# Encoder layer on one core: one VectorE instruction with the inverse rms, the shift inside the split, and the first instructions in another order

## The chip, the core and the metric

The kernel runs on one core of a Trainium2 chip. A core has TensorE (PE, the matrix unit; it loads 128x128 weights, which a profile shows as PEld, and writes to PSUM), VectorE (DVE), ScalarE (ACT), GpSimd (POOL) and SyncE (SP), whose queue issues all DMAs of this kernel. Each engine takes its instructions in the order of the program and waits on semaphores for the others. The metric is the device time of one execution in microseconds (us), lower is better.

## What is computed

One encoder layer for two groups of 1024 tokens, "prompt" and "sample", with 1024 channels, in fp32:

```python
mod = silu(c) @ w_ada + b_ada
shift, scale, gate = split(mod, 3)
h = rms_norm(x, norm_g) * (1.0 + scale) + shift          # the "modulated" rows
qa, ka, va, za, qb, kb, vb, zb, ga, gb = split(h @ w_in)
oa = gqa_attention(rope(rms_norm(qa)), rope(rms_norm(ka)), va) * silu(za)
ob = rms_norm(diff_attention(qb, kb, vb, lam)) * (1 - lam_init) * silu(zb)
merged = sigmoid(ga) * (oa @ w_proj_a) + sigmoid(gb) * (ob @ w_proj_b)
out = x + gate * (merged @ w_out)
```

`rms_norm(x)` is `x * rsqrt(mean(x*x) + eps) * g`. Scale and shift are one number per channel and group; the inverse rms is one number per token.

## The kernel before

**Layout and split.** The rows `x` come transposed: a tile holds 128 channels (a chunk, c = 0 to 7) by 512 tokens (`hf` = 0 or 1, the first or second half rows). Every fp32 matmul is made of three matmuls on numbers of reduced precision (fp32r): each operand is split into a high part (a ScalarE copy that rounds) and a low part (value minus high part), and hi·hi, hi·lo and lo·hi are added in PSUM. So `ht[hf]` is two lists of chunks, high and low, and a weight tile `w` has a high and a low half, made by `split_w`: ScalarE copies, then GpSimd subtracts, or VectorE for every other piece while `alone[0]` is true (outside attention).

**Start of the first group (`start`).** The modulation is made on PE out of eight 1 MB pieces of `w_ada` (`ada`, L324; the sum lies in a PSUM tile). `ada_end` copies a sum to SBUF (VectorE, L342), lays it out by channels with eight small matmuls (`laid`, L336), adds the bias (L348) and, for the scale, multiplies by norm_g (L352): the result is `modc`. There are four such sums: shift and scale of chunks 0 to 3, shift and scale of chunks 4 to 7. The inverse rms of the first half rows comes from squares (ScalarE, L272), sums on VectorE (L278 to L283), a matmul with ones and a power on GpSimd (`inv_rms`), and is spread over all partitions by `spread` (four transposes on PE, L308, and a copy on ScalarE, L310). Then the rows are multiplied by it (L394), scaled and shifted (`modulated`: L360 on VectorE or L358 on ScalarE), copied to the high part (L363) and subtracted for the low part (L364). The squares of the second half rows follow.

**Head.** `kva_gen` makes k and v of branch A for one tile of 128 tokens at a time (24 matmuls of 128x256, L539; then rms and rope of the row on VectorE, and a transpose of the row on PE, L593, two tiles later), and `z_gen` makes one z tile (24 matmuls of 128x512, L709). Tiles 0 to 3 use the first half rows, tiles 4 to 7 the second. `head` sets the order for the first group: tiles 0 and 1, one z tile, `late()` (inverse rms, spread and modulation of the second half rows, `start_late`: L412, L415, L416, L417), tiles 2 and 3, a second z tile, then the rest woven with query projections. After that attention and projections are woven by a table of shares.

**Second group.** `ht_gen` modulates the rows of the second group chunk by chunk, woven with the output projection `out_gen` of the first (L977): two VectorE instructions (L515), one GpSimd addition of the shift (L518), two high copies (L523) and two subtractions (L524) per chunk.

**What sets the order.** The code is written for all engines in one sequence; a scheduler then places each engine's instructions by its own estimate of times. `behind(a, b)` pins a behind b on one engine, and `tc.high_priority` raises some. A tile pool with a number of buffers makes a writer wait for the last reader of the buffer: `spool` has 3 buffers for weight pieces (`st`), `mtile("ev")` has one.

Of the kernel before, what the change touches and what calls it, by code (L numbers as in the profile page):

```python
# [12 lines left out]
F32 = mybir.dt.float32  # L13
F32R = mybir.dt.float32r
AF = mybir.ActivationFunctionType
# [5 lines left out]
P = 128  # L21
# [37 lines left out]
LAG = 2  # L59

# [28 lines left out]
def kernel(ctx: ExitStack, tc: tile.TileContext, t: dict):  # L89
# [99 lines left out]
    def split_w(w, q, st):  # L189
        wh = w[:, q * 2 : q * 2 + 2, 0, :]  # L190
        wl = w[:, q * 2 : q * 2 + 2, 1, :]
        nc.scalar.activation(wh, st, AF.Copy)  # L192
        e = nc.vector if alone[0] and q % 2 else nc.gpsimd
        e.tensor_tensor(out=wl, in0=st, in1=wh.bitcast(F32), op=ALU.subtract)  # L194

    def split_early(what):
        w, sts = what
        for q, st in enumerate(sts):
            split_w(w, q, st)
# [69 lines left out]
    def squares(xT):  # L269
        sq = [pair().rearrange("p (c n) -> p c n", c=4) for _ in range(2)]  # L270
        for c in range(NCH):
            nc.scalar.activation(sq[c // 4][:, c % 4], xT[c], AF.Square)  # L272
        return sq
# [30 lines left out]
    def spread(rs):  # L304

        bank = gbank()
        for k in range(4):
            nc.tensor.transpose(bank[:, k * P : (k + 1) * P], rs[:, k : k + 1].to_broadcast([P, P]), ident)  # L308
        rsb = mtile("ev", [P, 512], bufs=1)
        nc.scalar.activation(rsb, bank, AF.Copy)  # L310
        return rsb
# [26 lines left out]
    def ada_end(n):  # L338
# [3 lines left out]
        nc.vector.tensor_copy(row, acc)  # L342
# [8 lines left out]
        if third:  # L351
            nc.vector.tensor_tensor(out=mc, in0=mc, in1=gcol[:, cs].unsqueeze(2).to_broadcast(both), op=ALU.mult)  # L352

    def modulated(ht, hf, xT, cs):
        for c in cs:
            scale, shift = modc[:, 1, c, 0:1], modc[:, 0, c, 0:1]
            if c % 4 > 1:
                nc.scalar.activation(xT[c], xT[c], AF.Identity, scale=scale, bias=shift)  # L358
            else:
                nc.vector.tensor_scalar(  # L360
                    out=xT[c], in0=xT[c], scalar1=scale, scalar2=shift, op0=ALU.mult, op1=ALU.add
                )
            nc.scalar.activation(ht[hf][0][c], xT[c], AF.Copy)  # L363
            end = nc.vector.tensor_tensor(  # L364
                out=ht[hf][1][c], in0=xT[c], in1=ht[hf][0][c].bitcast(F32), op=ALU.subtract
            )
        return end
# [9 lines left out]
    def start(ht):  # L377
# [10 lines left out]
        for n in range(8):  # L388
            ada(n, wts[n])
            if n == 3:  # L390
                rsb = spread(inv_rms(added(squares(xT[0]))))
                for c in range(NCH):
                    e = nc.gpsimd if c % 3 == 2 else nc.vector
                    e.tensor_tensor(out=xT[0][c], in0=xT[0][c], in1=rsb, op=ALU.mult)  # L394
            if n in (2, 4, 6, 7):
                ada_end(n if n == 7 else n - 1)
            if n == 4:
                add_h(ht, 0, 0)
                modulated(ht, 0, xT[0], range(4))
        split_early(kva_w[0])  # L400
        add_h(ht, 0, 1)
        end = modulated(ht, 0, xT[0], range(4, 8))
        sq = squares(xT[1])
        return lambda: start_late(ht, xT, inv_rms(added(sq, end), latest[0]))

    def start_late(ht, xT, rs):
        rsb = spread(rs)
        for c in range(NCH):
            x = xT[1][c]
            if c % 4 == 0:  # L410
                add_h(ht, 1, c // 4)
            nc.vector.scalar_tensor_tensor(  # L412
                out=x, in0=x, scalar=modc[:, 1, c, 0:1], in1=rsb, op0=ALU.mult, op1=ALU.mult
            )
            nc.scalar.activation(x, x, AF.Identity, bias=modc[:, 0, c, 0:1])  # L415
            nc.scalar.activation(ht[1][0][c], x, AF.Copy)  # L416
            nc.vector.tensor_tensor(out=ht[1][1][c], in0=x, in1=ht[1][0][c].bitcast(F32), op=ALU.subtract)  # L417
# [71 lines left out]
    def ht_gen(g, ht):  # L489
# [20 lines left out]
        for c in range(NCH):  # L510
            xt = ptile()
            dma(xt, xT_in[g][c * P : (c + 1) * P])
            for hf in range(2):
                xh = xt[:, hf * 512 : (hf + 1) * 512]
                nc.vector.scalar_tensor_tensor(  # L515
                    out=xh, in0=xh, scalar=modc[:, 1, c, g : g + 1], in1=rsb[hf], op0=ALU.mult, op1=ALU.mult
                )
            nc.gpsimd.tensor_scalar(  # L518
                out=xt, in0=xt, scalar1=modc[:, 0, c, g : g + 1], scalar2=1.0, op0=ALU.add, op1=ALU.mult
            )  # L520
            for hf in range(2):
                xh = xt[:, hf * 512 : (hf + 1) * 512]
                nc.scalar.activation(ht[hf][0][c], xh, AF.Copy)  # L523
                nc.vector.tensor_tensor(out=ht[hf][1][c], in0=xh, in1=ht[hf][0][c].bitcast(F32), op=ALU.subtract)  # L524
# [465 lines left out]
    def head(g, st, zs, late):  # L990
# [3 lines left out]
        if g == 0:  # L994

            for i in range(2):
                drain(islice(kva, 6))
                drain(islice(zs, 3))
                if i == 0:
                    late()  # L1000
# [179 lines left out]
```

## Time and profile before

| | us |
|---|---|
| median of 3 runs | 1931.95 (1931.21 to 1932.6) |
| the profiled execution, its own time | 1934.43 |
| its span | 1932.7 |
| PE busy | 1863.8 |
| VectorE busy | 1161.5 |
| ScalarE busy | 760.0 |
| GpSimd busy | 674.2 |

A row of a timeline gives start, duration, engine, line, operation, output and inputs by the program's names, the count of merged instructions and, in brackets, how long the engine idled before and who released it. A row of windows gives the stretch, then busy time (count) of PE, its weight loads, VectorE, ScalarE and GpSimd, then PE's granted clock as a share of full speed, the DMA share and GB/s. The duration of a merged row runs from the first start to the last end.

### The profile page before, as it was taken

How to read it: one execution, taken by the hardware profiler on the slowest of the kernel's cores; microseconds unless marked ns; L12 is line 12 of the kernel's file. 1: busy time of each engine (PE TensorE's matmuls, PEld its weight loads, DVE VectorE, ACT ScalarE, POOL GpSimd, SP SyncE). 2: the span in 40 equal slices, each digit the busy share in tenths (PEclk: the TensorE clock that was granted, in tenths of full speed). 3: DMA queues.
4: the chain of work that ended last, by engine and by line, in shares of the span. 5: the costliest groups of instructions: out<-in, count | busy, mean ns of one | idle time of the engine just before them, and what ended most of it. 6: DMA issues, size and time to landing. Idle time of an engine off the chain costs nothing. (4 is left out here: it accounts for less than half of the span.)

```text
span 1932.7 us, 29441 instructions
## 1 busy us (share of the span) xinstructions
PE 1863.8 (96%) x10434; PEld 1562.7 (81%) x10434; DVE 1161.5 (60%) x1709; ACT 760.0 (39%) x1548; POOL 674.2 (35%) x912
## 2 busy tenths in 40 slices
PE   6989999999999998999999999999999899999999
PEld 3778878888888996788888777888888798877887
DVE  5787663444667366757467777445357736666731
ACT  4444442444445344323233455234445524442210
POOL 2233421433456254121222434024456616322110
PEclk8999999999999999999999999999999999999999
DMA  8136674546243355875631567564525423587531
GB/s 316 54 87 172 182 200 133 156 128 201 81 137 100 98 169 156 268 259 179 209 104 50 166 183 198 157 180 132 163 78 143 111 79 90 157 251 248 170 103 55
DMA packets 268883, 295.03 MB, mean 153 GB/s; under 512 B 35136, under 2 KB 217536, under 8 KB 268736
## 3 DMA queue, kind: packets, MB, share of 16 engines
q1 hardware_dynamic: 268736, 293.15, 51.0%
q8 instruction: 83, 1.36, 0.3%
q14 instruction: 64, 0.52, 0.1%
HBM read 133.59 MB, written 42.01 MB: 91 GB/s over the span
## 5 line engine op out<-in xcount | busy, mean ns | idle before, releaser
L709 PE MATMUL f<-u,w 128*128 128x512 f32 x2256 | 588.4, 398 | 1.3 <-ACT w L192 0.9
L539 PE MATMUL f<-w,u 128*128 128x256 f32 x3456 | 484.0, 286 | 1.9 <-DVE ev L719 0.9
L709 PEld LDWEIGHTS f<-u,w 128*128 128x128 f32 x2256 | 415.2, 190 | 85.2 <-issue 2.7
L539 PEld LDWEIGHTS f<-w,u 128*128 128x128 f32 x3456 | 456.8, 192 | 24.2 <-issue 2.7
L745 DVE TENSOR_REDUCE m<-s 128x1 f32<-128x1024 f32 x256 | 309.9, 1218 | 208.3 <-PE s L744 205.9
L746 ACT ACTIVATE p<-s,m 128x1024 f32<-128x1024 f32 x256 | 285.2, 1115 | 287.4 <-DVE m L745 219.2
L194 POOL TENSOR_TENSOR w<-st,w 128x512 fp32r<-128x512 f32 x168 | 223.0, 1345 | 455.9 <-ACT w L192 415.4
L787 DVE STREAM_TRANSPOSE p<-p 128x1024 f32<-128x1024 f32 x192 | 237.0, 1240 | 69.0 <-ACT p L746 59.3
L560 POOL TENSOR_TENSOR rs<-ss,nhalf 128x4 f32<-128x4 f32 (+1 forms) x112 | 109.1, 975 | 361.7 <-DVE ss L559 317.8
L744 PE MATMUL s<-u,sw 128*128 128x512 f32 x512 | 204.8, 400 | 0.0
L192 ACT ACTIVATE w<-st 128x512 fp32r<-128x512 f32 x196 | 115.1, 626 | 147.1 <-DMA st<-in_w_in_dram 92.2
L946 PE MATMUL f<-u,w 128*128 128x512 f32 x552 | 137.4, 398 | 3.9 <-DVE u L957 3.2
L819 PE MATMUL a<-q,u 128*128 128x256 f32 x512 | 132.8, 394 | 8.0 <-DMA q<-p 5.5
L946 PEld LDWEIGHTS f<-u,w 128*128 128x128 f32 x552 | 103.7, 190 | 27.4 <-DVE u L957 4.8
L819 PEld LDWEIGHTS a<-q,u 128*128 128x128 f32 x512 | 98.6, 198 | 24.9 <-issue 5.9
L802 PE MATMUL a<-q,u 128*64 128x256 f32 x1024 | 117.6, 382 | 1.0 <-DMA q<-p 1.0
L743 PE MATMUL s<-u 128*128 128x512 f32 x256 | 108.0, 422 | 10.2 <-ACT p L746 8.9
L596 DVE TENSOR_TENSOR u<-f,u 64x256 fp32r<-64x256 f32 (+1 forms) x196 | 80.6, 411 | 58.1 <-ACT u L595 53.1
L743 PE MATMUL s<-u,u 128*128 128x512 f32 x256 | 104.9, 410 | 8.4 <-DVE ev L719 4.3
L744 PEld LDWEIGHTS s<-u,sw 128*128 128x128 f32 x512 | 97.4, 190 | 17.5 <-issue 0.8
L977 PE MATMUL f<-u,w 128*128 128x512 f32 x456 | 105.6, 389 | 0.0
L786 DVE SCALAR_TENSOR_TENSOR p<-p,r,p 128x1024 f32<-128x1024 f32 x64 | 87.2, 1362 | 28.8 <-POOL r L772 24.2
(168 smaller groups left out, 1939.7 us busy)
## 6 DMA issues: line engine op xcount, KB each, us to landing
q<-p SPq DMA_DIRECT2D x768, 128.0 KB, 2.6
st<-in_w_in_dram SPq DMA_DIRECT2D x132, 256.0 KB, 3.1
zd<-ev SPq DMA_DIRECT2D x96, 256.0 KB, 2.6
sw<-u SPq DMA_DIRECT2D x256, 64.0 KB, 2.0
p<-zd SPq DMA_DIRECT2D x64, 256.0 KB, 4.1
u<-in_w_ada_dram SPq DMA_DIRECT2D x8, 1024.0 KB, 11.4
od<-oo SPq DMA_DIRECT2D x64, 128.0 KB, 2.4
st<-in_w_in_dram SPq DMA_DIRECT2D x64, 128.0 KB, 2.8
```

The source lines that it names most:

```text
L192: nc.scalar.activation(wh, st, AF.Copy)
L194: e.tensor_tensor(out=wl, in0=st, in1=wh.bitcast(F32), op=ALU.subtract)
L539: ins = nc.tensor.matmul(ps, lt[c][:, sl], w[:, c, wi, :], start=(k == 0), stop=(k == 23))
L709: ins = nc.tensor.matmul(ps, w[:, c, wi, e * P : (e + 1) * P], rt[c], start=(k == 0), stop=(k == 23),)
L743: nc.tensor.matmul(s[:, sl], q, k[:, sl], start=True, stop=False)
L744: nc.tensor.matmul(s[:, sl], sw, k[:, sl], start=False, stop=True)
L745: nc.vector.tensor_reduce(out=m, in_=s, axis=AX.X, op=ALU.max, negate=True)
L746: nc.scalar.activation(pt.rearrange("p (j c a) -> p j c a", j=4, c=8), s.rearrange("p (c a j) -> p j c a", c=8, j=4), AF.Exp, bias=m, accu ...
L787: nc.vector.transpose(pt, pt)
L802: lambda k=k, m=m: nc.tensor.matmul(acc[(LO, HI)[m]], u["v"][:, k], pT[m][:, k], start=(k == 0), stop=(k == 7))
L819: nc.tensor.matmul(acc, u["v"][:, k], pT[:, k], start=(k == 0), stop=(k == 7))
L946: nc.tensor.matmul(ps, w[:, c, wi, d * P : (d + 1) * P], o[:, oi, :], start=(k == 0), stop=(k == 11))
```

## The change

For every chunk and half, `modulate` writes three instructions that are bound to the engines' order: on VectorE x * scale * inverse rms in one instruction; on ScalarE the high part, rounded out of x + shift; on VectorE the low part, (x + shift) - high part. The low part of a chunk is pinned behind the next chunk's first instruction. It takes the place of `modulated` and the loop L394 in `start`, of the loop in `start_late`, and of the loops in `ht_gen`. The shift is no longer added by an instruction of its own.

Besides, `late` is now two steps (`FIRST`): the inverse rms of the second half rows behind the first z tile, their spread and modulation behind tiles 2 and 3; the spread is pinned behind the last matmul written before it, z matmuls included. The squares of the second half rows are pinned two by two behind the high parts of the first half's chunks 4 to 7, and the VectorE splits of the k/v weights behind the last copy of the modulation sums.

```diff
+FIRST = (("kva", 6), ("z", 3), ("late", 0), ("kva", 6), ("late", 1), ("z", 3))
...
-    def split_w(w, q, st):
+    def split_w(w, q, st, after=None):
...
-        e.tensor_tensor(out=wl, in0=st, in1=wh.bitcast(F32), op=ALU.subtract)
+        ins = e.tensor_tensor(out=wl, in0=st, in1=wh.bitcast(F32), op=ALU.subtract)
+        if after is not None and e is nc.vector:
+            behind(ins, after)
...
-    def squares(xT):
+    def squares(xT, after=None):
...
+            if after is not None:
+                behind(ins, after[c // 2])
...
-    def spread(rs):
+    def spread(rs, after=None):
...
+            if after is not None:
+                behind(ins, after)
...
-    def modulated(ht, hf, xT, cs):
...
+    def modulate(ht, hf, xs, rsb, g=0):
+
+        acts = []
+
+        def low(c, x):
+            hi, lo = (part[c] for part in ht[hf])
+            return nc.vector.scalar_tensor_tensor(
+                out=lo, in0=x, scalar=modc[:, 0, c, g : g + 1], in1=hi.bitcast(F32), op0=ALU.add, op1=ALU.subtract
+            )
+
+        prev, ins = None, None
+        for c, x in xs + [(None, None)]:
+            if x is not None:
+                new = nc.vector.scalar_tensor_tensor(
+                    out=x, in0=x, scalar=modc[:, 1, c, g : g + 1], in1=rsb, op0=ALU.mult, op1=ALU.mult
+                )
+                if ins is not None:
+                    behind(new, ins)
+                ins = new
+                acts.append(nc.scalar.activation(ht[hf][0][c], x, AF.Identity, bias=modc[:, 0, c, g : g + 1]))
+            if prev:
+                new = low(*prev)
+                behind(new, ins)
+                ins = new
+            prev = c, x
+        return ins, acts
...
                 rsb = spread(inv_rms(added(squares(xT[0]))))
-                for c in range(NCH):
-                    e = nc.gpsimd if c % 3 == 2 else nc.vector
-                    e.tensor_tensor(out=xT[0][c], in0=xT[0][c], in1=rsb, op=ALU.mult)
             if n in (2, 4, 6, 7):
-                ada_end(n if n == 7 else n - 1)
+                copied = ada_end(n if n == 7 else n - 1)
             if n == 4:
                 add_h(ht, 0, 0)
-                modulated(ht, 0, xT[0], range(4))
-        split_early(kva_w[0])
+                modulate(ht, 0, list(enumerate(xT[0]))[:4], rsb)
+        split_early(kva_w[0], copied)
         add_h(ht, 0, 1)
-        end = modulated(ht, 0, xT[0], range(4, 8))
-        sq = squares(xT[1])
-        return lambda: start_late(ht, xT, inv_rms(added(sq, end), latest[0]))
+        end, acts = modulate(ht, 0, list(enumerate(xT[0]))[4:], rsb)
+        sums = added(squares(xT[1], acts), end)
+        rs = []
+        return lambda: rs.append(inv_rms(sums, latest[0])), lambda: start_late(ht, xT, rs[0])

     def start_late(ht, xT, rs):
-        rsb = spread(rs)
...
+        rsb = spread(rs, latest[0])
+        for half in range(2):
+            add_h(ht, 1, half)
+            modulate(ht, 1, list(enumerate(xT[1]))[half * 4 : half * 4 + 4], rsb)
...
                         if col == C_ZA and hf == e == k == 0 and alone[0]:
                             behind(ins, latest[0])
+                        if alone[0]:
+                            latest[0] = ins
```

Line numbers after the change lie a few to some twenty lines further on (L342 is L349, L348 and L352 are L355 and L359, L194 is L195, L539 is L540, L709 is L710, L308 is L313, L310 is L317); L375 is the new first instruction, L381 the high part and L368 the low part.

On VectorE in `start`, before, between the first copy of a modulation sum (`p` from PSUM `s` or `f`) and the modulation of chunks 4 to 7 (`u_168`; `u_167` holds chunks 0 to 3, `ev_253` the spread inverse rms, `u_278` the low parts):

```order
L342 COPY p_268<-s_207 128x512
L394 TENSOR_TENSOR u_167<-u_167,ev_253 128x512 x3
L394 TENSOR_TENSOR u_168<-u_168,ev_253 128x512 x3
L348 TENSOR_TENSOR modc<-s_270,bcol 128x8
L342 COPY p_300<-f_263 128x512
L352 TENSOR_TENSOR modc<-modc,gcol 128x8
L360 TENSOR_SCALAR u_167<-u_167,modc 128x512 x2
L364 TENSOR_TENSOR u_278<-u_167,u_277 128x512 x3
L348 TENSOR_TENSOR modc<-f_302,bcol 128x8
L364 TENSOR_TENSOR u_278<-u_167,u_277 128x512
L194 TENSOR_TENSOR w_185<-p_186,w_185 128x2x256
L342 COPY p_312<-f_295 128x512
```

and the same place now (`u_270` holds the low parts, `w_185` is the k/v weight):

```order
L355 TENSOR_TENSOR modc<-s_262,bcol 128x8
L359 TENSOR_TENSOR modc<-modc,gcol 128x8
L375 SCALAR_TENSOR_TENSOR u_167<-u_167,modc,ev_253 128x512 x2
L349 COPY p_292<-f_255 128x512
L368 SCALAR_TENSOR_TENSOR u_270<-u_167,modc,u_269 128x512
L375 SCALAR_TENSOR_TENSOR u_167<-u_167,modc,ev_253 128x512
L368 SCALAR_TENSOR_TENSOR u_270<-u_167,modc,u_269 128x512
L375 SCALAR_TENSOR_TENSOR u_167<-u_167,modc,ev_253 128x512
L368 SCALAR_TENSOR_TENSOR u_270<-u_167,modc,u_269 128x512 x2
L355 TENSOR_TENSOR modc<-f_294,bcol 128x8
L349 COPY p_304<-f_287 128x512
L195 TENSOR_TENSOR w_185<-p_186,w_185 128x2x256
```

The six multiplications are gone from in front of the scale's sum, and the weight splits (the second one comes next) stand behind the last copy of a sum, where one stood ahead of it.

On PE, before, from the end of the first z tile (`f_461`) to tiles 2 and 3 (`f_548`, `f_595`); `row_…` are rows to be transposed, `rs_501` is the inverse rms of the second half rows:

```order
L291 MATMUL s_495<-ones_c,q_343 128x1 x4
L709 MATMUL f_461<-u_329,w_444 128x512 x2
L709 MATMUL f_461<-u_330,w_444 128x512
L709 MATMUL f_461<-u_329,w_444 128x512
L593 MATMUL s_636<-ident,row_428 128x128
L308 MATMUL f_505<-ident,rs_501 128x128 x4
L539 MATMUL f_548<-w_185,u_277 128x256 x2
L539 MATMUL f_548<-w_185,u_278 128x256
```

and now, in the middle of the second z tile (`f_626`; tile 2 is done before the first z tile ends, tile 3 behind it):

```order
L710 MATMUL f_626<-u_270,w_440 128x512
L710 MATMUL f_626<-u_269,w_440 128x512
L313 MATMUL s_591<-ident,rs_493 128x128 x4
L710 MATMUL f_626<-u_321,w_440 128x512
L710 MATMUL f_626<-u_322,w_440 128x512
```

The spread of the second half rows' inverse rms has moved from ahead of tiles 2 and 3 to behind the 12th matmul of the second z tile. Behind that tile, on PE now, tiles 4 (`f_656`) and 5 (`f_703`) begin, which use the second half rows (`u_598` high, `u_599` low):

```order
L594 MATMUL s_697<-ident,row_522 128x128
L540 MATMUL f_656<-w_185,u_598 128x256 x2
L540 MATMUL f_703<-w_185,u_598 128x256 x2
L540 MATMUL f_656<-w_185,u_599 128x256
L540 MATMUL f_656<-w_185,u_598 128x256 x2
L540 MATMUL f_703<-w_185,u_599 128x256
L540 MATMUL f_703<-w_185,u_598 128x256 x2
L540 MATMUL f_656<-w_185,u_599 128x256
L540 MATMUL f_703<-w_185,u_599 128x256
L540 MATMUL f_656<-w_185,u_598 128x256 x2
L540 MATMUL f_703<-w_185,u_598 128x256 x2
L540 MATMUL f_656<-w_185,u_599 128x256
```

Both tiles go through the chunks together, and the last row of these is the low part of chunk 2.

On VectorE now, the modulation of the second half rows (`u_192` and `u_193` hold chunks 0 to 3 and 4 to 7, `u_599` and `u_613` the low parts), behind the rope of tile 3 (`row_569`):

```order
L375 SCALAR_TENSOR_TENSOR u_192<-u_192,modc,ev_596 128x512 x2
L375 SCALAR_TENSOR_TENSOR u_193<-u_193,modc,ev_596 128x512 x2
L583 TENSOR_TENSOR row_569<-rc_580,row_569 128x128
L368 SCALAR_TENSOR_TENSOR u_599<-u_192,modc,u_598 128x512
L375 SCALAR_TENSOR_TENSOR u_192<-u_192,modc,ev_596 128x512
L368 SCALAR_TENSOR_TENSOR u_599<-u_192,modc,u_598 128x512
L375 SCALAR_TENSOR_TENSOR u_192<-u_192,modc,ev_596 128x512
L597 TENSOR_TENSOR u_356<-s_697,u_356 64x128
L368 SCALAR_TENSOR_TENSOR u_613<-u_193,modc,u_612 128x512
```

The two halves of four chunks are interleaved: chunks 0, 1, 4 and 5 are multiplied before the first low part, and the low part of chunk 2 comes behind 6 and 7.

More of the change, by code (lines that the diff above doesn't have):

```diff
@@ L352, in ada_end @@
             nc.vector.tensor_tensor(out=mc, in0=mc, in1=gcol[:, cs].unsqueeze(2).to_broadcast(both), op=ALU.mult)
[L354 to L367 removed]
+        return ins
+    def modulate(ht, hf, xs, rsb, g=0):
[10 more added lines that the diff above has]
+                    out=x, in0=x, scalar=modc[:, 1, c, g : g + 1], in1=rsb, op0=ALU.mult, op1=ALU.mult
+                )
+                if ins is not None:
[8 more added lines that the diff above has]
+        return ins, acts
     kva_w = []
@@ L513, in ht_gen @@
             for hf in range(2):
[L514 to L524, printed above, removed]
+                modulate(ht, hf, [(c, xt[:, hf * 512 : (hf + 1) * 512])], rsb[hf], g)
             yield 1
@@ L994, in head @@
         if g == 0:
[L996 to L1000, printed above, removed]
+            for what, n in FIRST:
+                if what == "late":
+                    late[n]()
+                else:
+                    drain(islice(kva if what == "kva" else zs, n))
             weave((chain(kva, qa), 40, 0.0), (islice(zs, nz - 6), nz - 6, Z_HEAD_A[g]))
```

20 lines of the change are left out of this document (5 added, 15 removed).

## The prediction

> **What bounds the kernel.** I read the page first, then busy time by windows, then the timelines of TensorE, VectorE and ScalarE over the first 90 us and around 990 us.
>
> ```profile
> PE 1863.8 (96%) x10434; PEld 1562.7 (81%) x10434; DVE 1161.5 (60%) x1709; ACT 760.0 (39%) x1548; POOL 674.2 (35%) x912
> 30.00:40.00 10.00, 6.03 (x27) 4.31 (x28) 7.79 (x15) 7.26 (x14) 3.25 (x2) 0.51 1.08 358
> 50.00:60.00 10.00, 7.07 (x33) 5.43 (x34) 7.54 (x27) 2.71 (x4) 4.04 (x5) 0.87 0.43 136
> 90.00:100.00 10.00, 10.00 (x73) 9.40 (x72) 6.32 (x19) 3.76 (x11) 3.49 (x4) 1.00 0.43 132
> 990.00:1000.00 10.00, 10.00 (x70) 9.30 (x69) 5.59 (x9) 3.43 (x9) 4.90 (x4) 1.00 0.30 104
> ```
>
> TensorE (PE) is busy 96% of the span; the window rows give span, PE, its weight loads, VectorE, ScalarE, GpSimd, granted clock. PE has all it can do from 90 us on and at 990 us, so time can be won only before that, where it idles or its clock is below 1 (0.51 and 0.87 in two of the rows). What counts is how far earlier PE gets through the same work. My mark is the end of the matmuls of k/v tiles 4 and 5, which both programs reach with the same two z tiles behind them. Before, it is 79.80:
>
> ```profile
> 72.81 3.36 PE L539 MATMUL f<-w,u 128*128 128x256 f32 x23
> 76.55 3.25 PE L539 MATMUL f<-w,u 128*128 128x256 f32 x25 [0.27 <-DVE ev L719]
> 84.39 0.30 PE L593 MATMUL f<-ident,row 128*128 128x128 f32 x1 [1.04 <-DVE row L582]
> ```
>
> The 1.04 us wait behind it hangs on tile 4's own result, so it moves with the mark.
>
> **First half rows, chunks 0 to 3.** Removed: six VectorE and two GpSimd multiplications by rms (L394), and the separate shift.
>
> ```profile
> 23.95 5.85 DVE L394 TENSOR_TENSOR u<-u,ev 128x512 f32<-128x512 f32 x6 [0.95 <-ACT ev L310]
> 24.23 1.05 PE L336 MATMUL s<-pick,p 128*128 128x2 f32 x8
> 29.72 0.15 DVE L348 TENSOR_TENSOR modc<-s,bcol 128x8 f32<-128x8 f32 x1
> 34.60 0.68 DVE L364 TENSOR_TENSOR u<-u,u 128x512 fp32r<-128x512 f32 x1
> 60.84 5.39 DVE L412 SCALAR_TENSOR_TENSOR u<-u,modc,ev 128x512 f32<-128x512 f32 x8 [2.79 <-ACT ev L310]
> 65.09 1.33 ACT L415 ACTIVATE u<-u,modc 128x512 f32<-128x512 f32 x2
> ```
>
> The scale was laid out at 25.28 (24.23 + 1.05), but VectorE picked it up only at 29.72, behind L394. Now it picks it up at once: modc and its product with norm_g end near 25.7. The new three-operand instruction has no row with the shift as scalar; nearest is L412, (5.39 - 0.75)/7 = 0.66 us from start to start, the lower bound L364's 0.61 (same operands without a scalar), the upper 0.75 (no overlap). I take 0.66. ScalarE's high part with the shift as bias is L415's form: 0.72 us, 0.61 from start to start. Eight instructions of 0.66 and one copy of 0.61 from 25.7, with 0.3 of waiting for the last high part, end at 31.9. Before, the last low part ended at 35.28.
>
> **Chunks 4 to 7.** The last copy of the modulation sum follows at 31.95 + 0.68; the last piece of w_ada has landed (the fourth of the transposed-x issues, which waits for it, is out by 29.52). In the order the two k/v weight splits follow it and no longer stand ahead of it.
>
> ```profile
> 24.93 4.59 SPq L258 DMA_DIRECT2D u<-in_xT_prompt_dram  x4
> 35.31 1.64 DVE L194 TENSOR_TENSOR w<-p,w 128x512 fp32r<-128x512 f32 x1
> 36.88 0.68 DVE L342 COPY p<-f 128x512 f32<-128x512 f32 x1
> 37.48 1.16 DVE L194 TENSOR_TENSOR w<-p,w 128x512 fp32r<-128x512 f32 x1
> 37.70 1.84 PE L336 MATMUL s<-pick,p 128*128 128x2 f32 x8 [3.44 <-DVE p L342]
> 39.78 0.17 DVE L352 TENSOR_TENSOR modc<-modc,gcol 128x8 f32<-128x8 f32 x1
> 43.48 1.14 ACT L272 ACTIVATE q<-u 128x512 f32<-128x512 f32 x2
> 45.17 0.69 DVE L364 TENSOR_TENSOR u<-u,u 128x512 fp32r<-128x512 f32 x1 [0.71 <-ACT u L363]
> 47.15 0.63 PE L709 MATMUL f<-u,w 128*128 128x512 f32 x2
> ```
>
> So PE lays the columns out at 32.7 to 34.5 (1.84) under the splits (1.64 + 1.16, from 32.5 to about 35.5), and chunk 4 starts at 35.9 instead of 39.98: 4.1 us earlier. Then ScalarE sets the pace, since two squares of the second half rows (0.52 each) now stand behind each high part: 0.61 + 2 x 0.52 = 1.65 a chunk. High part 4 ends at 35.9 + 0.75 + 0.77 = 37.4, high part 7 at 42.4, the last low part at 43.1 (45.86 before). The squares end at 43.35, the first z weight piece is split by 44.0, and the first z matmul starts there and not at 47.15: 3.1 us earlier. ScalarE does 16 activations in place of 28 here and in the second half rows; the 12 that go (L358, L363, L415, L416) are already left out of these chains.
>
> **First z tile, tiles 2 and 3.** Tile 2 now stands on PE behind two z matmuls and covers the weight splits.
>
> ```profile
> 45.79 0.43 SPq L446 DMA_DIRECT2D p<-in_lam_k_dram  x1
> 46.78 1.36 POOL L194 TENSOR_TENSOR w<-st,w 128x512 fp32r<-128x512 f32 x1 [8.70 <-ACT w L192]
> 48.17 6.57 SPq L216 DMA_DIRECT2D st<-in_w_in_dram  x4
> 52.65 0.63 ACT L192 ACTIVATE w<-st 128x512 fp32r<-128x512 f32 x1 [3.20 <-DMA st<-in_w_in_dram]
> 53.67 0.67 DVE L194 TENSOR_TENSOR w<-st,w 128x512 fp32r<-128x512 f32 x1
> 54.71 1.19 PE L709 MATMUL f<-u,w 128*128 128x512 f32 x4
> 57.60 0.45 PE L593 MATMUL s<-ident,row 128*128 128x128 f32 x1 [1.71 <-DVE row L582]
> 58.38 1.11 PE L308 MATMUL f<-ident,rs 128*128 128x128 f32 x4 [0.33 <-POOL rs L301]
> 64.39 3.12 PE L539 MATMUL f<-w,u 128*128 128x256 f32 x24
> 67.34 5.63 PE L709 MATMUL f<-u,w 128*128 128x512 f32 x24
> ```
>
> The fourth z piece could be issued only at 48.17, when GpSimd freed its buffer, and was there at 52.65. Now GpSimd is done with it at 45.4 (44.0 + 1.36), and SyncE's queue with the small loads ahead at 46.2 (45.79 + 0.43): landing 50.6, high part to 51.3, split on VectorE by 52.0 (54.34 before), z tile done at 53.0 (55.90). The row transpose behind it waits for a rope: before, the ropes of tiles 0 and 1 ran together from 54.34 to 57.60; tile 0 now goes first, and I take two thirds, until 54.2. Tile 3 takes 3.1, until 57.4; the second z tile 5.6 and the spread of the inverse rms 0.6 (1.11 at half clock): 63.8, with a short transpose. Before, the same work ended at 67.34 + 5.63 = 72.97. That is 9 us, and most is given back in the next step.
>
> **Second half rows.** The spread (L308) now stands behind the 12th matmul of the second z tile, at 60.4 on PE; with ScalarE's copy it is there at 61.6. VectorE is at the ropes of tiles 2 and 3 until about 61.7 (57.4 plus some 4.3: tile 4's matmuls ended at 79.80 and its row was ready 4.6 later, at 84.39). So these eight chunks start at 61.7, not at 60.84, 0.9 us late. On VectorE the low part of chunk 2 has 12 of the new instructions and two rope steps ahead of it: 13 x 0.66 + 0.5 = 9.1, done at 70.8; the last low part at 73.0 (before: 77.09). PE has done 16 of tiles 4 and 5's 48 matmuls by 67.2, waits 3.6 us for that low part, and has 32 to do.
>
> ```profile
> 59.14 5.38 PE L539 MATMUL f<-w,u 128*128 128x256 f32 x24
> 62.00:64.00 2.00, 2.00 (x12) 2.00 (x11) 2.00 (x4) 0.00 (x0) 0.00 (x0) 0.50 0.00 0
> 76.41 0.68 DVE L417 TENSOR_TENSOR u<-u,u 128x512 fp32r<-128x512 f32 x1
> ```
>
> A matmul of this form takes 3.12/24 = 0.130 us at full clock and 5.38/24 = 0.224 at half. After the 1.71 and 0.33 us of waiting at 57.6 the clock stood at 0.50 until past 64, some 5 us of work. After 3.6 us I expect the same: 20 matmuls in 4.5 us and 12 in 1.6, end at 70.8 + 6.1 = 76.9. That is 2.9 us ahead of 79.80. At full clock it would be 75.0 (4.8 ahead), at half clock throughout 78.0 (1.8).
>
> [...]
>
> **The second group's rows (950 to 995 us).** Per chunk VectorE keeps four instructions (two of 0.61 become 0.66, together 0.9 us over eight chunks), and GpSimd loses eight of 1.13 to 2.02.
>
> ```profile
> L518 POOL TENSOR_SCALAR p<-p,modc x8: 1129/1132/2022, 947.7 to 992.3; 128x1024 f32<-128x1024 f32 x8
> 988.55 5.60 PE L977 MATMUL f<-u,w 128*128 128x512 f32 x24
> 993.99 8.79 PE L539 MATMUL f<-w,u 128*128 128x256 f32 x72
> ```
>
> PE runs out_gen's matmuls until 994.15 and goes on without a wait. Shorter chunk chains cannot make it start sooner; I cost this part at nothing. If the last low part came over 1 us later than its 995.3, PE would wait by as much; GpSimd's stop on the chain is gone, so it comes earlier.
>
> **Order further on.** From about PE's 620th matmul (150 us) to 300 us, and from 1095 to 1250 us, z, projection and score matmuls are shuffled. There PE hardly waits before, so there is nothing to win: 0 to 2 us may be lost, by the size of one such wait at the start of attention.
>
> ```profile
> 134.83 0.50 PE L743 MATMUL s<-u,u 128*128 128x512 f32 x1 [2.61 <-DVE ev L719]
> ```
>
> I take 0, as most scores keep their distance from what they wait for.
>
> **Sum.** -2.9 us on the profiled execution's span of 1932.7; its time (1934.43) lies 2.5 above the median of the runs, 1931.95, which I shift alike: 1929.0, 0.15% faster. A difference of 0.2% (3.9 us) is about what a measurement tells from none.
>
> **Rivals.**
> 1. More gain: the clock holds, or the ropes end so that chunk 0 starts at 61.0. The mark falls at 75.0 or earlier: 1927.1 down to 1925. For it: PE is busy again at 64 to 67; against it: the drop at 57.6 after a shorter wait. Chance 0.30.
> 2. Nothing left: PE is short of work around 43.5, so the clock falls there as well, tile 2 runs at half (24 x 0.09 = 2.3 us, of which PE's wait for the fourth z piece covers 0.7), and the rest follows: chunk 0 at 63.3, mark at 78.5, 1930.7. For it: PE works on chunks 4 to 7 in pieces of 0.7 us every 1.65. Chance 0.15.
> 3. Slower: the spread, queued behind z matmuls, becomes the wait. The mark is chunk 0's start plus 15.2; with 64.6 nothing is gained, and 68.5 costs 3.9 (1935.9). This needs the first z tile to end 7 us later than 53.0, for instance if its fourth piece landed at 57 and not at 50.6; its 4.5 us of landing time at 48.17 speaks against it. Chance 0.06; a loss of that size from the shuffled order gets 0.04.
>
> **Numbers.** My forecast has 0.45, own range 1927.5 to 1930.5; a quarter of it may lie beyond -0.2%. Faster by over 0.2%: 0.30 + 0.10; within: 0.35 + 0.15; slower: 0.10. The range for 8 in 10 reaches from rival 1's better end, 1925.0, past rival 2 with one lost wait of 2.5: 1933.5.
>
> **What would show it.** In the profile after: low part 3 near 32, chunk 4 near 36, the first z matmul at 44, no half clock at 57 to 64, the second spread near 60.5, PE waiting some 3 us for VectorE's low part near 67 to 71 at a clock then near 0.5, the mark near 77; 990 to 1000 us unchanged. I am wrong if the ropes free VectorE much before or after 61.7, or if the attention stage shows new waits of PE.

## The result: 0.5% slower, and the profile after

| | before | after |
|---|---|---|
| median of 5 runs | 1932.60 (1931.21 to 1933.39) | 1942.19 (1937.79 to 1942.97) |
| span of the profiled execution | 1932.7 | 1940.4 |
| TensorE busy | 1863.8 | 1866.7 |
| VectorE busy | 1161.5 | 1160.9 |
| GpSimd busy | 674.2 | 658.8 |

The ratio is 1.0048, with a 95% interval of 1.0033 to 1.0062. The forecast was 1929.0, range 1925.0 to 1933.5: the time is 8.7 us above the range. The text said that the kernel would gain a little, and it lost.

First the windows, before and then after (span, then busy time of TensorE, its weight loads, VectorE, ScalarE and GpSimd, granted clock, DMA share, GB/s), cut where the second group's k/v tiles begin (about 994 us) and around 1200 us:

```profile
0.00:994.00 994.00, 949.82 (x5306) 791.65 (x5307) 614.31 (x909) 404.68 (x819) 347.33 (x468) 0.98 0.54 163
994.00:1180.00 186.00, 180.32 (x1147) 152.96 (x1146) 138.96 (x258) 80.98 (x190) 68.50 (x81) 0.98 0.46 131
1180.00:1240.00 60.00, 58.95 (x358) 48.01 (x357) 34.44 (x38) 26.96 (x53) 14.87 (x15) 1.00 0.69 197
```

```profile
0.00:994.00 994.00, 949.48 (x5319) 791.75 (x5320) 613.64 (x911) 404.95 (x810) 333.03 (x459) 0.98 0.54 163
994.00:1180.00 186.00, 179.63 (x1141) 152.04 (x1141) 140.77 (x256) 81.33 (x190) 68.04 (x81) 0.98 0.47 132
1180.00:1240.00 60.00, 54.83 (x323) 43.67 (x323) 28.88 (x33) 21.99 (x44) 14.62 (x15) 0.94 0.64 180
```

By 994 us the changed kernel has 13 matmuls more behind it, 5319 against 5306. The loss stands in the third row: between 1180 and 1240 us TensorE does 35 matmuls fewer, idles 4.1 us more (58.95 - 54.83), and works at 0.94 of the clock, which costs another 3.3 (54.83 x 0.06). It is the attention of the second group; all rows that the change modulates are done by 995 us.

A simple cut gives the same account. The start of the 72 matmuls for the second group's k/v tiles lies at 993.99 before, and after at 992.40:

```profile
992.40 8.79 PE L540 MATMUL f<-w,u 128*128 128x256 f32 x72
```

The change has gained 1.6 us by then. From there to the end of the span it takes 948.0 us (1940.4 - 992.40), where it took 938.7 (1932.7 - 993.99): 9.3 us lost, of which the third window explains 7.4. Of the other 1.9, 1.5 stand in one group of 24 k/v matmuls, before (first row) at a granted clock of 1.00, after (second row) at 0.66. They follow a wait of TensorE of 2.13 us before and 2.77 us after:

```profile
1547.23 3.11 PE L539 MATMUL f<-w,u 128*128 128x256 f32 x24
```

```profile
1552.33 4.61 PE L540 MATMUL f<-w,u 128*128 128x256 f32 x24
```

This part is not tied to the new order: in experiments 8 and 10 below, with the later order of the kernel before, the same 24 matmuls take 4.43 and 4.36 us, and in experiments 6 and 9, with that of the kernel after except around 1200 us, 3.12. I call the time up to the 72 matmuls the first stretch and the rest the second.

**The early part** does nearly what the prediction said up to the first z matmul, and loses time behind it. VectorE and then TensorE, timelines of the kernel after:

```profile
30.47 1.62 DVE L368 SCALAR_TENSOR_TENSOR u<-u,modc,u 128x512 fp32r<-128x512 f32 x2
...
35.77 1.42 DVE L375 SCALAR_TENSOR_TENSOR u<-u,modc,ev 128x512 f32<-128x512 f32 x2
...
62.94 2.73 DVE L375 SCALAR_TENSOR_TENSOR u<-u,modc,ev 128x512 f32<-128x512 f32 x4
...
71.53 1.41 DVE L368 SCALAR_TENSOR_TENSOR u<-u,modc,u 128x512 fp32r<-128x512 f32 x2
```

```profile
43.85 0.73 PE L710 MATMUL f<-u,w 128*128 128x512 f32 x2 [0.27 <-ACT w L193]
...
52.53 1.92 PE L710 MATMUL f<-u,w 128*128 128x512 f32 x6 [1.01 <-ACT w L193]
...
72.32 6.71 PE L540 MATMUL f<-w,u 128*128 128x256 f32 x32 [2.86 <-DVE u L368]
```

Low part 3 ends at 32.09 (forecast 31.9), chunk 4 starts at 35.77 (35.9), the first z matmul at 43.85 (44.0). The mark, the end of k/v tiles 4 and 5, is 72.32 + 6.71 = 79.03: 0.8 us ahead of the 79.80 before, where 2.9 had been forecast.

**The stop.** Timelines of TensorE, VectorE, ScalarE and SyncE's queue in the kernel after, around 1190 us:

```profile
1194.38 0.39 PE L747 MATMUL s<-u,sw 128*128 128x512 f32 x1
1199.93 0.79 PE L746 MATMUL s<-u,u 128*128 128x512 f32 x1 [5.17 <-ACT p L749]
...
1206.51 3.57 PE L710 MATMUL f<-u,w 128*128 128x512 f32 x15
```

```profile
1193.77 1.22 DVE L748 TENSOR_REDUCE m<-s 128x1 f32<-128x1024 f32 x1 [1.17 <-PE s L747]
```

```profile
1193.22 0.63 ACT L193 ACTIVATE w<-st 128x512 fp32r<-128x512 f32 x1 [1.34 <-DMA st<-in_w_in_dram]
1194.48 1.22 ACT L193 ACTIVATE w<-st 128x512 fp32r<-128x512 f32 x2 [0.63 <-DMA st<-in_w_in_dram]
...
1198.16 0.63 ACT L193 ACTIVATE w<-st 128x512 fp32r<-128x512 f32 x1 [1.92 <-DMA st<-in_w_in_dram]
1198.69 1.10 ACT L749 ACTIVATE p<-s,m 128x1024 f32<-128x1024 f32 x1
```

```profile
1179.57 8.78 SPq L799 DMA_DIRECT2D q<-p  x12
...
1189.09 1.48 SPq L219 DMA_DIRECT2D st<-in_w_in_dram  x3
...
1195.24 0.37 SPq L219 DMA_DIRECT2D st<-in_w_in_dram  x1
```

Read from the bottom: the four pieces of one weight tile are issued at 1189.09 (three) and 1195.24 (the fourth, which needs one of the three `spool` buffers back), behind twelve transfers of the attention. ScalarE's copies of them (L193) wait for each landing, and the exponential of a score (L749) stands behind the fourth copy, at 1198.69. The maximum that it needs (L748 on VectorE) was ready at 1194.99 (1193.77 + 1.22), so it starts 3.7 us after its own input. TensorE waits 5.17 us for the score's PSUM bank that this exponential frees. The matmuls of a z tile with weights long in SBUF (L710, 1206.51) stand behind that score. The kernel before has the same work there in another order:

```profile
1177.31 0.53 SPq L216 DMA_DIRECT2D st<-in_w_in_dram  x1
...
1179.27 10.31 SPq L796 DMA_DIRECT2D q<-p  x15
...
1195.72 1.23 PE L539 MATMUL f<-w,u 128*128 128x256 f32 x9
1196.78 2.23 PE L709 MATMUL f<-u,w 128*128 128x512 f32 x9
```

```profile
1195.78 1.12 ACT L746 ACTIVATE p<-s,m 128x1024 f32<-128x1024 f32 x1
...
1196.89 0.62 ACT L192 ACTIVATE w<-st 128x512 fp32r<-128x512 f32 x1
```

The first piece goes out ahead of the attention's transfers. On TensorE k/v and z matmuls follow at once, at 1195.72, and the score comes behind them; on ScalarE the exponential of the same score (L746) stands ahead of the copy of the tile's fourth piece (L192), not behind it.

### The profile page after: what moved, and what is told of

Same layout as the page of the kernel before. It is cut to its first block, busy times and chain, and to the rows that moved or that the text cites. A ratio compares the mean times of both kernels' runs of the same rounds, so it can differ in the third digit from the quotient of the medians.

```text
span 1940.4 us, 29407 instructions
## 1 busy us (share of the span) xinstructions
PE 1866.7 (96%) x10434; PEld 1565.0 (81%) x10434; DVE 1160.9 (60%) x1707; ACT 758.8 (39%) x1536; POOL 658.8 (34%) x902
## 5 line engine op out<-in xcount | busy, mean ns | idle before, releaser
L710 PE MATMUL f<-u,w 128*128 128x512 f32 x2256 | 587.5, 397 | 1.3 <-ACT w L193 1.3
L540 PE MATMUL f<-w,u 128*128 128x256 f32 x3456 | 491.3, 288 | 6.9 <-DVE u L368 4.5
L540 PEld LDWEIGHTS f<-w,u 128*128 128x128 f32 x3456 | 461.4, 194 | 31.5 <-DVE u L368 5.9
L710 PEld LDWEIGHTS f<-u,w 128*128 128x128 f32 x2256 | 413.5, 189 | 85.7 <-issue 3.1
L748 DVE TENSOR_REDUCE m<-s 128x1 f32<-128x1024 f32 x256 | 310.7, 1219 | 207.6 <-PE s L747 205.0
L195 POOL TENSOR_TENSOR w<-st,w 128x512 fp32r<-128x512 f32 x168 | 222.5, 1343 | 505.4 <-ACT w L193 481.4
L749 ACT ACTIVATE p<-s,m 128x1024 f32<-128x1024 f32 x256 | 285.3, 1115 | 274.2 <-DVE m L748 212.6
L193 ACT ACTIVATE w<-st 128x512 fp32r<-128x512 f32 x196 | 114.7, 626 | 152.5 <-DMA st<-in_w_in_dram 90.7
L746 PE MATMUL s<-u 128*128 128x512 f32 x256 | 108.5, 424 | 10.1 <-ACT p L749 10.1
L746 PE MATMUL s<-u,u 128*128 128x512 f32 x256 | 105.3, 411 | 13.4 <-ACT p L749 7.7
```

Source lines behind the costliest of these rows:

```text
L195: ins = e.tensor_tensor(out=wl, in0=st, in1=wh.bitcast(F32), op=ALU.subtract)
L540: ins = nc.tensor.matmul(ps, lt[c][:, sl], w[:, c, wi, :], start=(k == 0), stop=(k == 23))
L710: ins = nc.tensor.matmul(ps, w[:, c, wi, e * P : (e + 1) * P], rt[c], start=(k == 0), stop=(k == 23),)
L746: nc.tensor.matmul(s[:, sl], q, k[:, sl], start=True, stop=False)
L748: nc.vector.tensor_reduce(out=m, in_=s, axis=AX.X, op=ALU.max, negate=True)
L749: nc.scalar.activation(pt.rearrange("p (j c a) -> p j c a", j=4, c=8), s.rearrange("p (c a j) -> p j c a", c=8, j=4), AF.Exp, bias=m, accu ...
```

## The experiments

Theory 1: the loss is the second group's order; the early part by itself gains. Rival 2: the new instructions cost it. Rival 3: no early lead can reach the end. All ratios are against the kernel before, in runs on the same chip; TensorE's order below always means the sequence of its instructions in the built program. The two stretches of an experiment come from one execution each, and executions scatter: 33 of the kernel before, on one chip, lie between 1928.67 and 1940.91. So a difference of two or three us in one stretch decides nothing by itself.

**Experiment 1: chunk by chunk.**

```diff
-            modulate(ht, 1, list(enumerate(xT[1]))[half * 4 : half * 4 + 4], rsb)
+            for c in range(half * 4, half * 4 + 4):
+                modulate(ht, 1, [(c, xT[1][c])], rsb)
```

> The changed kernel, in which the second half rows of the first group are modulated chunk by chunk: the low part of a chunk is no longer pinned behind the next chunk's first instruction. With it TensorE's first 450 instructions stand as in the changed kernel, and from there to the end as in the kernel before. Theory 1 (the loss is the other order of the second group's attention, in which TensorE stops for 5.2 us near 1195 us; the early part is a gain): the stop at 1195 is gone and the early lead of some 3 us stays, 1929 to 1931 us. Rival 2 (the loss comes with the new instructions themselves, above all those of the second group's rows): 1938 to 1942. Rival 3 (no lead can reach the end: the transfers near 1190 us keep their time and take it back): 1932 to 1934, with a wait of about 3 us there.

Measured: 1931.93, ratio 0.9992 (0.9980 to 1.0003). The profiled span is 1927.3, first stretch to 989.83, second 937.5. Here, and in the next, nothing longer than 0.9 us is left of TensorE's waits between 1100 and 1260 us (the longest of TensorE's waits: total, times, longest one; experiment 1, then 2):

```profile
PE a L806 <- DMA q<-p: 0.8, 1, 0.8
```

```profile
PE a L805 <- DMA q<-p: 0.9, 1, 0.9
```

The stop is gone with the order, and all new instructions are still there, so rival 2 is out. The median is 0.9 us above the expected range, and its ratio cannot be told from none: the early gain is smaller than theory 1 had it, if there is one.

**Experiment 2: spread and modulation ahead of tile 3.**

```diff
-FIRST = (("kva", 6), ("z", 3), ("late", 0), ("kva", 6), ("late", 1), ("z", 3))
+FIRST = (("kva", 6), ("z", 3), ("late", 0), ("kva", 3), ("late", 1), ("kva", 3), ("z", 3))
```

> The changed kernel, in which the spread and the modulation of the second half rows stand ahead of tile 3 and no longer behind it. TensorE's order is that of the kernel before from its 500th instruction on, and within the first 350 a little different from both. Theory 1: no stop at 1195 us; the early lead is 2 to 4 us, so 1928.5 to 1931. Rival 2 (new instructions): 1938 to 1942. Rival 3 (the lead is taken back at 1190): 1932 to 1934.

Measured: 1930.19, ratio 0.9983 (0.9974 to 0.9992): faster than both kernels, by 0.17% than the one before. First stretch to 987.52, second 940.7. VectorE starts on chunk 0 at 60.34 and not at 62.94:

```profile
60.34 0.75 DVE L375 SCALAR_TENSOR_TENSOR u<-u,modc,ev 128x512 f32<-128x512 f32 x1 [0.84 <-ACT ev L317]
```

So the changed kernel's own place for the spread, behind the 12th matmul of the second z tile, costs 2.6 us at this point. And rival 3 is out as it stands: no wait of 3 us is left near 1190 us, and the whole interval of the ratio lies below 1.

**Experiment 3: the squares free.**

```diff
-        sums = added(squares(xT[1], acts), end)
+        sums = added(squares(xT[1]), end)
```

> The changed kernel without the pins of the squares of the second half rows. TensorE's order is that of the kernel before from the 450th instruction to the 5000th, and that of the changed kernel in the second group's attention. Theory 1 in its narrow form (the order of the second group's attention is the loss, the shuffle at 150 to 300 us costs nothing): the stop near 1195 us is there as in the changed kernel, 1939 to 1943. A rival (the shuffle at 150 to 300 us is what costs): 1929 to 1933.

Measured: 1941.10, ratio 1.0039 (1.0024 to 1.0053), with the stop. The shuffle at 150 to 300 us is not the loss. TensorE's waits from 1100 to 1260 us, here and in experiment 4:

```profile
PE s L746 <- ACT p L749: 5.6, 1, 5.6
```

```profile
PE s L756 <- ACT p L759: 4.7, 1, 4.7
```

**Experiment 4: the second group's rows as before.** The call of `modulate` in `ht_gen` is replaced by the old body (scale and inverse rms, GpSimd's addition of the shift, two copies, two subtractions).

> The changed kernel, with the rows of the second group modulated as before (scale and inverse rms, shift on GpSimd, two copies, two subtractions). TensorE's order is that of the changed kernel throughout. Theory 1: nothing changes, 1939 to 1943, with the stop near 1195 us. Rival 2 (the new instructions of the second group's rows cost the time): 1929 to 1934.

Measured: 1940.90, ratio 1.0036 (1.0022 to 1.0050), second stretch 947.4. Without the new instructions of these rows the loss is all there, as theory 1 had it.

**Experiment 5: the late weight tile on GpSimd's queue.** The number names that one tile.

```diff
+        start = nc.gpsimd.dma_start if uid[0] == 1896 else dma
...
-                dma(st[:, :, off : off + n], src.rearrange("(c p) n -> p c n", p=P))
+                start(st[:, :, off : off + n], src.rearrange("(c p) n -> p c n", p=P))
```

> The changed kernel, in which the transfers of one weight tile (the one whose four pieces land between 1193 and 1198 us) are issued on GpSimd's queue and not behind the attention's transfers on SyncE's. The early part and TensorE's order up to that place stay those of the changed kernel; from there to about 1260 us the scheduler places the z and k/v matmuls of that stretch as the kernel before has them. Theory 1 (what is lost is the stop near 1195 us: an exponential stands on ScalarE behind copies of weight pieces that are not there yet, and TensorE has no projection matmul ahead of the score that waits for it): the stop of 5.2 us and the low clock after it (2.8 us) shrink to about 1 us, 1942 becomes 1934 to 1937. Rival (that stop only shows a delay that the second group has anyway): the loss moves on to the next units, 1940 to 1943.

Measured: 1937.74, ratio 1.0019 (1.0007 to 1.0032), between the two theories. The score no longer waits; a row does. TensorE and GpSimd:

```profile
1196.17 0.69 PE L595 MATMUL f<-ident,row 128*128 128x128 f32 x2 [3.43 <-POOL row L584]
```

```profile
1191.72 1.29 POOL L195 TENSOR_TENSOR w<-st,w 128x512 fp32r<-128x512 f32 x1 [3.07 <-ACT w L193]
1192.96 0.73 POOL L660 TENSOR_TENSOR row<-row,gqa 128x256 f32<-128x256 f32 x1
```

GpSimd stood 3.07 us in front of the fourth piece, with that row's rope queued behind it.

**Experiment 6: z matmuls ahead of the score.** The z tile's matmuls (number 1903) are written under a higher scheduling priority and the score (number 1929) is pinned behind the 18th of them, which `held[0]` keeps; the transfers stay.

```diff
+                        with (tc.high_priority(offset=60) if here == 1903 else nullcontext()):
...
+            if here == 1929 and n == 0:
+                behind(ins, held[0])
```

> The changed kernel, in which TensorE gets 18 matmuls of a z tile, whose weights have long been there, ahead of the score on which it stops near 1195 us; all transfers stay on SyncE's queue, so the weight pieces still land at 1193 to 1198 us and ScalarE's copies still wait for them. Theory 1: TensorE has 4 us of work for the wait of 5.2, but 12 k/v matmuls with the late weights stand ahead of it, so some 2 us of waiting stay: 1936 to 1939. Rival (the stop is only where a delay shows): 1940 to 1943.

Measured: 1941.11, ratio 1.0040 (1.0027 to 1.0053): the expectation failed. TensorE:

```profile
1195.31 0.44 PE L595 MATMUL f<-ident,row 128*128 128x128 f32 x2 [1.66 <-POOL row L584]
1195.50 0.36 PE L541 MATMUL f<-w,u 128*128 128x256 f32 x1
1196.53 0.85 PE L541 MATMUL f<-w,u 128*128 128x256 f32 x5 [0.66 <-POOL w L196]
1197.85 0.38 PE L541 MATMUL f<-w,u 128*128 128x256 f32 x1 [0.47 <-ACT w L194]
1199.20 2.71 PE L541 MATMUL f<-w,u 128*128 128x256 f32 x11 [0.96 <-POOL w L196]
1202.95 7.10 PE L715 MATMUL f<-u,w 128*128 128x512 f32 x24 [1.04 <-DVE u L598]
```

Five waits, 4.8 us together, on a row, on the weights' pieces and on VectorE's work on that row, take the place of one. The k/v matmuls with the late weights stand ahead of the z matmuls that were to cover them. So the score was only the first in line. That the weight tile is what is late is tested in experiment 9.

**Experiment 7: the new rows of the second group alone.** The kernel before, with `modulate` in `ht_gen`.

> The kernel before, with the new three instructions for the rows of the second group alone. TensorE's order is that of the kernel before throughout. Theory 1: no change, 1931.5 to 1934, since TensorE runs the output projection beside these rows. Rival 2 (these instructions cost or save time by themselves): beyond 2 us from the kernel before, either way.

Measured: 1933.40, ratio 1.0000 (0.9986 to 1.0014). Nothing gained or lost, as costed, to within the interval.

**Experiment 8: the new rows of the first group alone.** The kernel before, with `modulate` in `start` and in `start_late`; splits, squares and the late step as they were.

> The kernel before, with the new three instructions for the rows of the first group, but all early work where it was: splits, squares and the late step as before. TensorE's order differs from that of the kernel before in 37 of the first 500 instructions and nowhere else. Theory 1: VectorE's chain for chunks 0 to 3 is 3.4 us shorter and that of the second half rows, from 60.84 us on, some 3 us; the lead is smaller than the 3 us of the changed kernel's early part or like it, with no stop at 1195 us: 1929.5 to 1932.5. If the early order is what the lead comes from, nothing is gained: 1932 to 1934.

Measured: 1937.24, ratio 1.0019 (1.0005 to 1.0032): slower, which neither expectation had. TensorE is early, reaches the end of its matmuls for tile 7 at 82.9, and stands there:

```profile
87.39 0.45 PE L610 MATMUL f<-ident,row 128*128 128x128 f32 x1 [4.34 <-DVE row L599]
87.49 4.19 PE L726 MATMUL f<-u,w 128*128 128x512 f32 x9
```

VectorE has the rows of the last tiles still to do; the lead turns into a wait of 4.34 us and nine matmuls at about half the pace (4.19 us, 0.47 each; 22 took 5.26 before, 0.24 each). The granted clock from 80 to 90 us is 0.75, where it was 1.00 before. The first stretch ends at 995.61, 1.6 later than before. A shorter modulation alone is worth less than nothing here. The second stretch is 3.1 us longer as well (941.8); 1.3 of that is the group of 24 matmuls of the result section, which is slow here too (4.43 us against 3.11). What the rest is, these runs don't tell.

**Experiment 9: the late weight tile earlier on SyncE's own queue.**

```diff
+        early_dma = uid[0] == 1896
...
+                with tc.high_priority(offset=400) if early_dma else nullcontext():
+                    dma(st[:, :, off : off + n], src.rearrange("(c p) n -> p c n", p=P))
```

> The changed kernel, in which the transfers of the weight tile that lands at 1193 to 1198 us stand earlier on SyncE's own queue; GpSimd's queue is left as it was. Theory 1 in its narrow form (what TensorE runs out of near 1190 us are these weights: the score, the row and the k/v matmuls that it stopped on in the earlier experiments all stood behind them or behind ScalarE's and GpSimd's work on them): no wait over 1 us is left there, and the time is 1934 to 1936.5, as the lead of some 1 to 3 us stays and about 2 us of low clock near 1540 us are still lost. Rival (in this order TensorE runs dry there for several reasons, and each repair shows the next one): a wait of 2 to 5 us on something else, 1937 to 1941.

Measured: 1932.99, ratio 0.9998 (0.9989 to 1.0007): the loss is gone through one tile's four transfers, and the time is 1 us below the range that theory 1 gave. Of a lead over the kernel before nothing shows. SyncE's queue, then all of TensorE's waits from 1085 to 1270 us:

```profile
1184.96 0.55 SPq L222 DMA_DIRECT2D st<-in_w_in_dram  x1
```

```profile
PE s L749 <- ACT p L752: 0.6, 2, 0.5
PE f L543 <- ACT u L698: 0.4, 1, 0.4
```

The fourth piece is out at 1184.96, not at 1195.24. The second stretch is 939.9. TensorE's order differs from that of the changed kernel in 131 of 9524 places, all within this stretch, so the repair is of the transfers and of what the scheduler then places around them.

**Experiment 10: the spread in tile 3, the squares free.** `FIRST` as in experiment 2 with 4 and 2 steps of k/v in place of 3 and 3, and the edit of experiment 3.

> The changed kernel, with the squares of the second half rows free and the spread behind the first third of tile 3's matmuls. TensorE's order is that of the kernel before from about the 500th instruction on. By theory 1 there is no stop near 1195 us, and the time is that of the kernel before less the early lead: tile 3 covers the 1.7 us for which TensorE waited for the inverse rms in the experiment with the spread ahead of tile 3, but the free squares give the fourth z piece's copy away, so the lead is 2 to 5 us, 1928 to 1931. If the stop comes with the early lead and not with the order: 1938 to 1942.

Measured: 1933.17, ratio 1.0001 (0.9992 to 1.0011). The stop is gone, so it does not come with the early lead. But the expected 1928 to 1931 is missed by 2 us: the first stretch ends at 989.69, 4.3 us ahead, the second takes 941.4, and in the median nothing of the lead is left. How much of an early lead reaches the end, these runs leave open. The first z tile is held up as in experiment 3, which also left the squares free (2.45 us there):

```profile
53.21 2.34 PE L710 MATMUL f<-u,w 128*128 128x512 f32 x6 [2.60 <-ACT w L193]
```

**Experiment 11: another order, nothing else.**

```diff
+                        with tc.high_priority(offset=0):
```

> The changed kernel with the z matmuls written under a scheduling priority of zero. No instruction is added, removed or changed, and the first 250 stay in place; but TensorE's order differs from then on in 3171 of 9524 places. Theory 1, in its general form (the order alone moves this kernel by more than the change's own gain): at least 3 us from the changed kernel's 1942, either way, with waits of TensorE in other places. Rival (the order is worth little, and the loss is tied to the one stop): within 3 us of 1935 if the stop is gone, of 1942 if it is there.

Measured: 1939.95, ratio 1.0034 (1.0024 to 1.0045), and the stop at 1195 is not there. The second stretch is 944.8. Waits have moved; over the whole span, the largest that the kernel after hardly has (0.4 us there) is that of the attention's values for VectorE's copy of the unit before:

```profile
PE a L823 <- DVE oo L829: 4.7, 3, 3.0
```

The time is 2.2 us from the changed kernel's, so the 3 us that the general form of theory 1 asked for were not reached, and the rival's 1935 was not either. What it shows: in a third order the waits come to a like sum, at other places.

## Why the prediction was wrong, point by point

**Chunks 0 to 7: right.** Low part 3, chunk 4, the first z matmul, and the last low part of this half, at 43.02 (43.1), all lay within 0.2 us.

**First z tile, second half rows: the mechanism right, the sizes off.** The first z tile ends at 54.45 (52.53 + 1.92), not at 53.0: the fourth piece was issued in time (45.75, forecast 46.2) but took 6.1 us to land where I had taken 4.4 (ScalarE's copy starts at 51.85, not at 50.6). Chunk 0 starts at 62.94 instead of 61.7, and the low part of chunk 2 is there at 72.3 instead of 70.8. TensorE waits 2.86 us for it, after 1.6 us in two waits shortly before (forecast 3.6), and then the granted clock stays at 0.50 until 78.0, so that the 32 matmuls take 6.71 us instead of 6.1. This adds up to 79.03 against 76.9, the place of rival 2, though the clock at 43 us was not the cause (1.00 from 40 to 47 us).

The term of -2.9 was too large, and whether anything of it is there is not shown. It was counted from 79.80, the mark of one execution, in which the clock stood at 0.50 from 60 to 64 us and tile 2 took 5.38 us. Experiment 7 leaves all early instructions of the kernel before as they were; in its profile TensorE's clock is 1.00 there, tile 2 takes 3.12 us, and the mark is at 76.50 (73.24 + 3.26):

```profile
58.10 3.12 PE L556 MATMUL f<-w,u 128*128 128x256 f32 x24
...
73.24 3.26 PE L556 MATMUL f<-w,u 128*128 128x256 f32 x25 [0.27 <-DVE ev L736]
```

So the mark moves by 3.3 us between two executions of the same early code, more than the whole term. Five profiles with the changed early code (after, experiments 4, 5, 6 and 9) have it between 78.08 and 79.38, and end the first stretch between 990.67 and 994.48, 992.2 on average; without that code (before, experiment 7) the stretch ends at 993.99 and 993.50. That is a lead of some 1.5 us, with a scatter of 3.8. In the times of experiment 9, which has this code and not the loss, no lead shows (0.9989 to 1.0007).

**The spread behind z matmuls: a rival that was partly true.** Experiment 2 starts the same eight chunks 2.6 us earlier and ends the first stretch 4.9 us earlier than the kernel after, in one profile of each. I gave the mechanism a threshold of a much later first z tile; it cost something without that.

**The second group's rows: right.** Experiments 4 and 7.

**"Order further on": the step that failed.** "I take 0, as most scores keep their distance from what they wait for", with 0 to 2 us as the bound. It measured 9.3 us in the profile, 1.5 of them by the clock near 1552 us, which is not tied to the order. Over all profiles it is some 8 us: with TensorE's later order of the kernel before (before, experiments 1, 2, 7, 8 and 10) the second stretch takes 937.5 to 941.8 us, with that of the kernel after (after, experiments 3 and 4) 947.4 to 949.0. I compared scores with their own inputs, and bounded a new wait by one at the start of attention. Neither looks at what is queued ahead on ScalarE and SyncE: the score's own inputs were on time, and its bank came late because of copies of weights for other matmuls. The list of what moved named the z and projection matmuls between 1095 and 1250 us; a check of which weight tile they need, and when its pieces are issued, could have led there. A loss of that size had 0.04.

I had also left open what caused the reshuffle. It is not the second group's rows: with the old ones (experiment 4) TensorE's order is that of the kernel after in every place, and with the new ones alone (experiment 7) that of the kernel before. It comes from the early edits, 1000 us ahead, by way of the scheduler's estimates. Which of them tips it was not settled: the squares' pins tip the shuffle at 150 to 300 us, but taking them away left the later one; chunk-wise modulation or an earlier spread tips both back.

## What to carry to other kernels

Where a scheduler orders the program by estimated times, an early edit may reorder a stage a thousand microseconds later, and that can outweigh the edit (here it cost some 8 us). So cost each reshuffled stretch on the queues of all engines: look for a load of weights that has slid behind other transfers, and for what stands behind its copies. And compare an edit in two or three programs whose later order differs: here much the same early part came out at 1942, 1933 and 1932 us (after, experiments 9 and 1). Before an early gain of a few us is counted, take the mark from more than one execution: here it moved by 3.3 us without any edit.

## What was not expected of the hardware

After nearly the same wait of TensorE for the low part of chunk 2, the same 32 matmuls took very different times: 6.61 us after 3.43 (experiment 9), 5.59 after 3.44 (experiment 4), 5.37 after 3.44 (experiment 3):

```profile
72.65 6.61 PE L543 MATMUL f<-w,u 128*128 128x256 f32 x32 [3.43 <-DVE u L371]
```

```profile
73.15 5.59 PE L550 MATMUL f<-w,u 128*128 128x256 f32 x32 [3.44 <-DVE u L368]
```

```profile
74.85 5.37 PE L540 MATMUL f<-w,u 128*128 128x256 f32 x32 [3.44 <-DVE u L368]
```

In experiment 10 they took 4.09 us after 3.22, at a granted clock of 1.00 throughout:

```profile
73.34 4.09 PE L540 MATMUL f<-w,u 128*128 128x256 f32 x32 [3.22 <-DVE u L368]
```

So in these profiles the length of one wait does not tell how long the clock stays low, or whether it falls. In the kernel after the 32 matmuls took 6.71 us after a wait of 2.86; there the clock had fallen already after the two waits before, of 1.26 and 0.34 us (1.00 from 64.0 to 67.9 us, 0.55 from 67.9 to 69.5, 0.50 from 72.3 to 78.0).

At the 24 k/v matmuls near 1552 us, shown with the result, the wait does separate the runs: in six profiles it is 1.64 to 2.21 us and they take 3.11 or 3.12 us, in six others (after, experiments 3, 4, 5, 8 and 10) it is 2.56 to 3.13 us and they take 4.36 to 4.61.
